# Mixture of softmaxes on one core: joint head weights, own buffers for the exponentials, and part loads of two heads

## Chip, core, metric

The kernel runs on one core of one Trainium2 chip. The metric is device time in microseconds (us) of one execution; each figure is the median of a kernel's runs. Each kernel ran in turns with the kernel before, on one chip. Three chips were used, with medians of the kernel before of 782.82, 782.70 and 782.74 us, and the control of the experiments (the changed kernel) ran on the first only; so where a run from another chip is set against the control, about 0.1 us of the difference may be the chip's. Two runs of one kernel mostly differ by 0.1 to 0.5 us.

## The reference

```python
def reference(logits, prior):            # logits (32, 128, 4, 4096), prior (32, 128, 4), float32
    prior_probs = softmax(prior, axis=-1)
    softmax = softmax(logits, axis=-1)   # over the vocabulary of 4096
    return np.sum(prior_probs[..., None] * softmax, axis=2)     # sum over the 4 heads
```

(The two softmaxes are written out in the original, with the maximum subtracted.) 268.5 MB come in and 67.1 MB go out.

## The kernel before

The 4096 rows are worked in 32 units of 128 rows. A unit loads 4 heads x 4096 values for each row (8.39 MB), takes exponentials on ScalarE, weights and adds them on VectorE, and stores 2.10 MB. There are two load buffers. Units 0 and 29 to 31 are loaded head by head, the others in one transfer.

```python
def pieces(b):
    return 1 if b == 0 or b >= B - 3 else H      # heads in one transfer
...
for b in range(B):
    ...
    if 0 < b < B - 3:
        store(b - 1, eng=nc.scalar)               # ahead of this unit's exponentials
    for h in range(H):
        et = lt[:, h] if inplace else ebuf[:, h % 2]          # two exponential buffers
        ex = nc.scalar.activation(et, lt[:, h], AF.Exp, accum_out=dsum[:, col])
        ...
        nc.vector.reciprocal(rden[:, col], dsum[:, col])      # one for each head
        if h == 0:
            nc.vector.tensor_scalar(out=acc, in0=et, scalar1=rden[:, col], scalar2=pp[...], ...)
            continue
        nc.gpsimd.tensor_mul(coeff[:, col], rden[:, col], pp[...])   # one for each head
        ...                                                   # last head of all: two halves
            nc.vector.scalar_tensor_tensor(out=acc[:, cs], in0=et[:, cs], scalar=coeff[:, col],
                                           in1=acc[:, cs], op0=ALU.mult, op1=ALU.add)
            if split:
                store(b, c * w, (c + 1) * w)
    if b + 2 < B:
        load(b + 2)                               # free once the four exponentials are done
```

The softmax here doesn't subtract the row's maximum and nothing guards it: scores larger than these inputs give would overflow.

Of the kernel before, what the change touches and what calls it, by code (L numbers as in the profile page):

```python
# [38 lines left out]
def kernel(  # L39
# [6 lines left out]
    nc = tc.nc  # L46
    B, S, H, V = logits.shape
    assert prior.shape == (B, S, H)
    assert out.shape == (B, S, V)
    P = 128  # L50
# [3 lines left out]
    B = G * J  # L54
    assert G * R == B * S and G <= 32

# [4 lines left out]
    lpool = ctx.enter_context(tc.tile_pool(name="lpool", bufs=2))  # L61
    apool = ctx.enter_context(tc.tile_pool(name="apool", bufs=2))
    cpool = ctx.enter_context(tc.tile_pool(name="cpool", bufs=1))


    def pieces(b):
        return 1 if b == 0 or b >= B - 3 else H

    ltiles = {}

    def load(b, eng=nc.sync):
        lt = lpool.tile([P, H, V], FP32, name="ltile")
        n = pieces(b)
        for h in range(0, H, n):
            eng.dma_start(out=lt[:, h : h + n], in_=lg[b // J, b % J, :, h : h + n, :])  # L75
        ltiles[b] = lt

    accs = {}

    def store(b, lo=0, hi=V, eng=nc.sync):  # L80
        eng.dma_start(out=ov[b // J, b % J, :, lo:hi], in_=accs[b][:, lo:hi])

    load(0, eng=nc.sync)
    nc.at_finalize(early_first_load)


    pr = cpool.tile([G, R, H], FP32, name="pr")
    nc.scalar.dma_start(out=pr, in_=pv)
    load(1, eng=nc.sync)
    pn = cpool.tile([32, H, R], FP32, name="pn")  # L90
    nc.gpsimd.memset(pn, 0.0)  # L91
    pmax = cpool.tile([G, R], FP32, name="pmax")
    nc.vector.reduce_max(pmax, pr, axis=AX.X)  # L93
    nc.vector.tensor_sub(pr, pr, pmax.unsqueeze(2).to_broadcast([G, R, H]))  # L94
    nc.scalar.activation(pr, pr, AF.Exp)  # L95
    nc.vector.reduce_sum(pmax, pr, axis=AX.X)  # L96
    nc.vector.reciprocal(pmax, pmax)  # L97
    nc.vector.tensor_mul(  # L98
        pn[0:G].rearrange("g h r -> g r h"), pr, pmax.unsqueeze(2).to_broadcast([G, R, H])
    )  # L100
    pq = pn.rearrange("g h (p j) -> g j h p", j=J)

    pp = cpool.tile([P, J, H, 32], FP32, name="pp")
    for t in range(P // 32):
        nc.vector.transpose(pp[32 * t : 32 * (t + 1)], pq[:, :, :, 32 * t : 32 * (t + 1)])  # L105

    NCHUNK = 2


    dsum = cpool.tile([P, B * H], FP32, name="dsum")  # L110
    rden = cpool.tile([P, B * H], FP32, name="rden")
    coeff = cpool.tile([P, B * H], FP32, name="coeff")


    ebuf = cpool.tile([P, 2, V], FP32, name="ebuf")

    exps = []

    for b in range(B):
        last = b == B - 1  # L120
        inplace = b >= B - 2
        lt = ltiles.pop(b)
        if not inplace:
            accs[b] = apool.tile([P, V], FP32, name="acc")
        else:
            accs[b] = lt[:, 0]
        acc = accs[b]
        if 0 < b < B - 3:
            store(b - 1, eng=nc.scalar)
        for h in range(H):  # L130
            split = last and h == H - 1
            i = b * H + h
            col = slice(i, i + 1)
            et = lt[:, h] if inplace else ebuf[:, h % 2]
            ex = nc.scalar.activation(et, lt[:, h], AF.Exp, accum_out=dsum[:, col])  # L135
            if h == 0:
                tc.keep_in_program_order(ex)


            if not inplace:  # L140
                if len(exps) >= 2:
                    tc.declare_no_dep(ex.ins, exps[-2], reason="covered by the sum")
                exps.append(ex.ins)
            nc.vector.reciprocal(rden[:, col], dsum[:, col])  # L144
            if h == 0:
                nc.vector.tensor_scalar(  # L146
                    out=acc, in0=et, scalar1=rden[:, col], scalar2=pp[:, b % J, h, b // J : b // J + 1],
# [51 lines left out]
```

## Time and profile before

| | |
|---|---|
| time, at first | 782.52 us (782.52 to 782.69, 3 runs) |
| span of the profiled run | 780.6 us |
| VectorE / ScalarE / POOL busy | 68% / 60% / 2% |
| transfers | nine tenths or more of every slice but the last |

The prediction below shows the lines and how to read them. The page's queue list: its columns are the queue and its kind, the packets, their MB, and their share of the 16 transfer engines' time.

```profile
q14 instruction: 7, 0.06, 0.0%
```

Seven packets of 8 KB each, in the whole run: instructions being fetched. 0.0% of the transfer time looks like nothing.

### The profile page before, as it was taken

The page shows a single profiled execution, that of the slowest core. Times are in us where ns is not written, and L with a number is a line of the kernel's source. Part 1 is how long each engine was busy: PE and PEld are TensorE (multiplying, and loading weights), DVE is VectorE, ACT ScalarE, POOL GpSimd, SP SyncE. Part 2 cuts the span into 40 slices and gives each one's busy share as a digit, 9 for nine tenths or more (in the row PEclk, how much of TensorE's full clock was granted, in tenths as well). Part 3 has the DMA queues.
Part 4 walks back from the last instruction along what each step waited for, and adds up shares of the span by engine and source line. Part 5 has one row for each costly group of instructions (what it writes and reads, how often), then busy time and mean ns, then how long its engine had stood idle before and what let it go on. Part 6 is the DMA issues. An engine that isn't in the chain of part 4 may idle for free.

```text
span 780.6 us, 853 instructions
## 1 busy us (share of the span) xinstructions
DVE 531.4 (68%) x266; ACT 470.2 (60%) x258; POOL 19.3 (2%) x101
## 2 busy tenths in 40 slices
DVE  5756668656686666866667765677666776668994
ACT  4376555755557655576555775457655567558971
POOL 0000000000000000000000000000000000000000
DMA  9999999999999999999999999999999999999998
GB/s 388 434 454 433 403 470 403 467 407 442 431 415 458 413 460 403 453 421 460 413 442 444 400 459 413 453 424 449 411 456 417 453 416 424 449 413 430 429 429 359
DMA packets 11127, 335.67 MB, mean 430 GB/s; under 512 B 1248, under 2 KB 1248, under 8 KB 1264
## 3 DMA queue, kind: packets, MB, share of 16 engines
q1 hardware_dynamic: 7056, 276.83, 82.2%
q10 hardware_dynamic: 4064, 58.79, 17.6%
q14 instruction: 7, 0.06, 0.0%
HBM read 268.50 MB, written 67.11 MB: 430 GB/s over the span
## 4 chain that ended last, share of the span: by engine, by line
DMA 66%; ACT 14%; DVE 10%; issue 7%; POOL 0%; SPq 0%; DVEq 0%; POOLq 0%; ACTq 0%
DMA ltile<-in_logits_dram 66%; ACT ebuf L135 14%; DVE acc L156 9%; DVE ltile L156 1%; POOL coeff L151 0%; SPq L75 0%; DVE rden L144 0%; DVEq L194 0%; DVE ltile L146 0%; POOLq L194 0%; ACTq L135 0%
## 5 line engine op out<-in xcount | busy, mean ns | idle before, releaser
L135 ACT ACTIVATE ebuf<-ltile 128x4096 f32<-128x4096 f32 x120 | 433.0, 3609 | 281.3 <-DMA ltile<-in_logits_dram 234.5
L156 DVE SCALAR_TENSOR_TENSOR acc<-ebuf,coeff,acc 128x4096 f32<-128x4096 f32 x90 | 403.6, 4484 | 27.3 <-POOL coeff L151 27.3
L144 DVE RECIPROCAL rden<-dsum 128x1 f32<-128x1 f32 x128 | 20.4, 160 | 200.7 <-ACT ebuf L135 200.7
L146 DVE TENSOR_SCALAR acc<-ebuf,rden,pp 128x4096 f32<-128x4096 f32 x30 | 72.4, 2412 | 1.1
L151 POOL TENSOR_TENSOR coeff<-rden,pp 128x1 f32<-128x1 f32 x96 | 18.2, 189 | 746.2 <-DVE rden L144 746.2
L135 ACT ACTIVATE ltile<-ltile 128x4096 f32<-128x4096 f32 x8 | 28.9, 3609 | 4.2 <-DMA ltile<-in_logits_dram 4.2
L156 DVE SCALAR_TENSOR_TENSOR ltile<-ltile,coeff 128x4096 f32<-128x4096 f32 (+1 forms) x7 | 27.0, 3874 | 1.8 <-POOL coeff L151 1.8
L135 ACT ACTIVATION_READ_ACCUMULATOR ebuf<-ltile 128x1 f32 x120 | 22.4, 186 | 0.0
L93 DVE TENSOR_REDUCE pmax<-pr 16x256 f32<-16x1024 f32 x1 | 1.2, 1207 | 7.0 <-DMA pr<-in_prior_dram 7.0
L95 ACT ACTIVATE pr<-pr 16x1024 f32<-16x1024 f32 x1 | 1.1, 1056 | 7.0 <-DVE pr L94 7.0
L146 DVE TENSOR_SCALAR ltile<-ltile,rden,pp 128x4096 f32<-128x4096 f32 x2 | 4.8, 2414 | 0.1
L98 DVE TENSOR_TENSOR pn<-pr,pmax 16x1024 f32<-16x1024 f32 x1 | 1.9, 1945 | 0.1
L95 ACT ACT_TABLE_LOAD x1 | 1.3, 1283 | 1.2 <-PEq L183 1.2
L96 DVE TENSOR_REDUCE pmax<-pr 16x256 f32<-16x1024 f32 x1 | 1.2, 1207 | 1.1 <-ACT pr L95 1.1
L105 DVE STREAM_TRANSPOSE pp<-pn 32x256 f32<-32x256 f32 x4 | 1.7, 435 | 0.1
L97 DVE RECIPROCAL pmax<-pmax 16x256 f32<-16x256 f32 x1 | 1.7, 1741 | 0.0
L135 ACT ACTIVATION_READ_ACCUMULATOR ltile<-ltile 128x1 f32 x8 | 1.5, 186 | 0.0
L94 DVE TENSOR_TENSOR pr<-pr,pmax 16x1024 f32<-16x1024 f32 x1 | 1.2, 1214 | 0.0
L91 POOL MEMSET pn<- 32x1024 f32 x1 | 0.9, 941 | 0.3 <-POOLq L183 0.3
L183 POOL MEMSET const-float32-0.0<- 128x1 f32 x1 | 0.1, 103 | 0.2 <-issue 0.2
L183 POOL MEMSET const-bfloat16-1.0<- 128x1 bf16 x1 | 0.1, 106 | 0.0
L183 POOL MEMSET const-uint8-127<- 128x1 uint8 x1 | 0.1, 106 | 0.0
(1 smaller groups left out, 0.1 us busy)
## 6 DMA issues: line engine op xcount, KB each, us to landing
out_dram<-acc ACTq DMA_DIRECT2D x28, 2048.0 KB, 29.3
ltile<-in_logits_dram SPq DMA_DIRECT2D x16, 2048.0 KB, 20.3
out_dram<-acc SPq DMA_DIRECT2D x2, 2048.0 KB, 32.9
out_dram<-ltile SPq DMA_DIRECT2D x1, 2048.0 KB, 21.2
out_dram<-ltile SPq DMA_DIRECT2D x2, 1024.0 KB, 8.7
ltile<-in_logits_dram SPq DMA_DIRECT2D x28, 32.3
pr<-in_prior_dram ACTq DMA_DIRECT2D x1, 64.0 KB, 6.2
```

The source lines that it names most:

```text
L93: nc.vector.reduce_max(pmax, pr, axis=AX.X)
L94: nc.vector.tensor_sub(pr, pr, pmax.unsqueeze(2).to_broadcast([G, R, H]))
L95: nc.scalar.activation(pr, pr, AF.Exp)
L96: nc.vector.reduce_sum(pmax, pr, axis=AX.X)
L97: nc.vector.reciprocal(pmax, pmax)
L98: nc.vector.tensor_mul(pn[0:G].rearrange("g h r -> g r h"), pr, pmax.unsqueeze(2).to_broadcast([G, R, H]))
L105: nc.vector.transpose(pp[32 * t : 32 * (t + 1)], pq[:, :, :, 32 * t : 32 * (t + 1)])
L135: ex = nc.scalar.activation(et, lt[:, h], AF.Exp, accum_out=dsum[:, col])
L144: nc.vector.reciprocal(rden[:, col], dsum[:, col])
L146: nc.vector.tensor_scalar(out=acc, in0=et, scalar1=rden[:, col], scalar2=pp[:, b % J, h, b // J : b // J + 1], op0=ALU.mult, op1=ALU.mult,)
L151: nc.gpsimd.tensor_mul(coeff[:, col], rden[:, col], pp[:, b % J, h, b // J : b // J + 1])
L156: nc.vector.scalar_tensor_tensor(out=acc[:, cs], in0=et[:, cs], scalar=coeff[:, col], in1=acc[:, cs], op0=ALU.mult, op1=ALU.add,)
```

## The change

Intent: fewer instructions and fewer waits. One reciprocal and one POOL product serve all four heads of a unit (two heads in the last four units). The first exponential is written in place, the other three have a buffer each (one in PSUM), so ScalarE does not wait for VectorE within a unit. A list of needed waits replaces those that the framework would insert. Loads in parts come as two heads, the last unit as two, one and one. The store of a unit now stands before the fourth exponential of the next one.

```diff
-        n = pieces(b)
-        for h in range(0, H, n):
-            eng.dma_start(out=lt[:, h : h + n], in_=lg[b // J, b % J, :, h : h + n, :])
+        if u == 0 or u >= U - 3:
+            cuts = (0, 2, 3, 4) if u == U - 1 else (0, 2, 4)
+        else:
+            cuts = (0, H)
+        for h, to in zip(cuts, cuts[1:]):
+            ld = nc.sync.dma_start(out=ltile[:, u % 2, h:to], in_=lg[u // J, u % J, :, h:to, :])
+            if u >= 2:
+                only(ld, adds[u - 2, 0] if h == 0 else exps[u - 2, to - 1])
 ... (cut: only() keeps just the named waits of an instruction)
-    ebuf = cpool.tile([P, 2, V], FP32, name="ebuf")
+    ebuf1 = cpool.tile([P, V], FP32, name="ebuf1")
+    ebuf2 = psum.tile([P, V], FP32, name="ebuf2")
+    ebuf3 = cpool.tile([P, V], FP32, name="ebuf3")
+            es = (lt[:, 0], ebuf1, ebuf2, ebuf3) if bufd else [lt[:, h] for h in range(H)]
 ...
-            nc.vector.reciprocal(rden[:, col], dsum[:, col])
-            nc.gpsimd.tensor_mul(coeff[:, col], rden[:, col], pp[:, b % J, h, b // J : b // J + 1])
+                rc = nc.vector.reciprocal(rden[:, u, h : h + n], dsum[:, u, h : h + n])
+                only(rc, exps[u, h + n - 1])
+                mul = nc.gpsimd.tensor_mul(
+                    coeff[:, u, h : h + n], rden[:, u, h : h + n], ppu[:, h : h + n]
+                )
 ...
+            m = H if u < U - 4 else 2                      # heads weighted together
+            for h in range(H):
+                if h == H - 1 and 0 < u < U - 3:
+                    store(u - 1, obuf[:, (u - 1) % 2], nc.scalar)
+                exp(h, ...)
+                if (h + 1) % m:
+                    continue
 ... (cut: weigh the m heads, add them one by one, last head of all in two halves)
```

More of the change, by code (lines that the diff above doesn't have):

```diff
@@ L46 @@
     nc = tc.nc
+    nc.at_finalize(early_first_load)
     B, S, H, V = logits.shape
@@ L53 @@
     G = B * S // R
-    B = G * J
-    assert G * R == B * S and G <= 32
+    U = G * J
+    assert G * R == B * S and G <= 32 and H == 4
     lg = logits.rearrange("b s h v -> (b s) h v").rearrange("(g p j) h v -> g j p h v", p=P, j=J)
@@ L59 @@
     pv = prior.rearrange("b s h -> (b s) h").rearrange("(g r) h -> g r h", r=R)
-    lpool = ctx.enter_context(tc.tile_pool(name="lpool", bufs=2))
-    apool = ctx.enter_context(tc.tile_pool(name="apool", bufs=2))
     cpool = ctx.enter_context(tc.tile_pool(name="cpool", bufs=1))
-    def pieces(b):
-        return 1 if b == 0 or b >= B - 3 else H
-    ltiles = {}
-    def load(b, eng=nc.sync):
-        lt = lpool.tile([P, H, V], FP32, name="ltile")
-        n = pieces(b)
-        for h in range(0, H, n):
-            eng.dma_start(out=lt[:, h : h + n], in_=lg[b // J, b % J, :, h : h + n, :])
-        ltiles[b] = lt
@@ L78, with only @@
-    accs = {}
-    def store(b, lo=0, hi=V, eng=nc.sync):
-        eng.dma_start(out=ov[b // J, b % J, :, lo:hi], in_=accs[b][:, lo:hi])
-    load(0, eng=nc.sync)
-    nc.at_finalize(early_first_load)
+    psum = ctx.enter_context(tc.tile_pool(name="psum", bufs=1, space=bass.MemoryType.PSUM))
+    before = {}
+    def only(ins, *keep):
+        for k in keep:
+            tc.add_manual_dep(
+                ins.ins,
+                k.ins.name,
+                mybir.DependencyInfo(mybir.DependencyClass.Sync, mybir.DependencyReason.DATA),
+                reason="all that this instruction waits for",
+            )
+        tc.declare_no_dep(
+            ins.ins,
+            group="loop",
+            keep=[k.ins for k in keep] + before.get(ins.ins.engine, []),
+            reason="covered by the waits that are kept",
+        )
+        tc.add_to_no_dep_group("loop", ins.ins)
+        before[ins.ins.engine] = [ins.ins]
+        return ins
@@ new lines, with load @@
+    ltile = cpool.tile([P, 2, H, V], FP32, name="ltile")
+    loads = {}
+    exps = {}
+    adds = {}
+    stores = {}
+    def load(u):
+        if u == 0 or u >= U - 3:
[3 more added lines that the diff above has]
+        for h, to in zip(cuts, cuts[1:]):
+            ld = nc.sync.dma_start(
+                out=ltile[:, u % 2, h:to], in_=lg[u // J, u % J, :, h:to, :]
+            )
+            if u >= 2:
+                only(ld, adds[u - 2, 0] if h == 0 else exps[u - 2, to - 1])
+            else:
+                only(ld)
+            for k in range(h, to):
+                loads[u, k] = ld
@@ L87, with store @@
+    def store(u, acc, eng, lo=0, hi=V):
+        st = eng.dma_start(out=ov[u // J, u % J, :, lo:hi], in_=acc[:, lo:hi])
+        stores[u] = only(st, adds[u, H - 1])
     pr = cpool.tile([G, R, H], FP32, name="pr")
-    nc.scalar.dma_start(out=pr, in_=pv)
-    load(1, eng=nc.sync)
     pn = cpool.tile([32, H, R], FP32, name="pn")
-    nc.gpsimd.memset(pn, 0.0)
     pmax = cpool.tile([G, R], FP32, name="pmax")
-    nc.vector.reduce_max(pmax, pr, axis=AX.X)
-    nc.vector.tensor_sub(pr, pr, pmax.unsqueeze(2).to_broadcast([G, R, H]))
@@ L95 @@
-    nc.scalar.activation(pr, pr, AF.Exp)
-    nc.vector.reduce_sum(pmax, pr, axis=AX.X)
-    nc.vector.reciprocal(pmax, pmax)
-    nc.vector.tensor_mul(
-        pn[0:G].rearrange("g h r -> g r h"), pr, pmax.unsqueeze(2).to_broadcast([G, R, H])
-    )
-    pq = pn.rearrange("g h (p j) -> g j h p", j=J)
-    pp = cpool.tile([P, J, H, 32], FP32, name="pp")
-    for t in range(P // 32):
-        nc.vector.transpose(pp[32 * t : 32 * (t + 1)], pq[:, :, :, 32 * t : 32 * (t + 1)])
-    NCHUNK = 2
-    dsum = cpool.tile([P, B * H], FP32, name="dsum")
@@ L111 @@
-    rden = cpool.tile([P, B * H], FP32, name="rden")
-    coeff = cpool.tile([P, B * H], FP32, name="coeff")
-    ebuf = cpool.tile([P, 2, V], FP32, name="ebuf")
-    exps = []
-    for b in range(B):
-        last = b == B - 1
-        inplace = b >= B - 2
-        lt = ltiles.pop(b)
-        if not inplace:
-            accs[b] = apool.tile([P, V], FP32, name="acc")
-        else:
-            accs[b] = lt[:, 0]
-        acc = accs[b]
-        if 0 < b < B - 3:
-            store(b - 1, eng=nc.scalar)
-        for h in range(H):
-            split = last and h == H - 1
-            i = b * H + h
-            col = slice(i, i + 1)
-            et = lt[:, h] if inplace else ebuf[:, h % 2]
-            ex = nc.scalar.activation(et, lt[:, h], AF.Exp, accum_out=dsum[:, col])
-            if h == 0:
-                tc.keep_in_program_order(ex)
-            if not inplace:
-                if len(exps) >= 2:
-                    tc.declare_no_dep(ex.ins, exps[-2], reason="covered by the sum")
-                exps.append(ex.ins)
-            nc.vector.reciprocal(rden[:, col], dsum[:, col])
-            if h == 0:
-                nc.vector.tensor_scalar(
-                    out=acc, in0=et, scalar1=rden[:, col], scalar2=pp[:, b % J, h, b // J : b // J + 1],
-                    op0=ALU.mult, op1=ALU.mult,
-                )
-                continue
-            nc.gpsimd.tensor_mul(coeff[:, col], rden[:, col], pp[:, b % J, h, b // J : b // J + 1])
-            n = NCHUNK if split else 1
-            w = V // n
-            for c in range(n):
-                cs = slice(c * w, (c + 1) * w)
-                nc.vector.scalar_tensor_tensor(
-                    out=acc[:, cs], in0=et[:, cs], scalar=coeff[:, col], in1=acc[:, cs],
-                    op0=ALU.mult, op1=ALU.add,
-                )
-                if split:
-                    store(b, c * w, (c + 1) * w)
-        if b + 2 < B:
-            load(b + 2)
-        if b == B - 3:
-            store(b - 1)
-            store(b)
-        elif b == B - 2:
-            store(b)
@@ new lines, with exp, weigh, add @@
+    pp = cpool.tile([P, J, H, 32], FP32, name="pp")
+    dsum = cpool.tile([P, U, H], FP32, name="dsum")
+    rden = cpool.tile([P, U, H], FP32, name="rden")
+    coeff = cpool.tile([P, U, H], FP32, name="coeff")
+    ebuf1 = cpool.tile([P, V], FP32, name="ebuf1")
+    ebuf2 = psum.tile([P, V], FP32, name="ebuf2")
+    ebuf3 = cpool.tile([P, V], FP32, name="ebuf3")
+    obuf = cpool.tile([P, 2, V], FP32, name="obuf")
+    with tc.manual_schedule():
+        load(0)
+        nc.scalar.dma_start(out=pr, in_=pv)
+        load(1)
+        nc.gpsimd.memset(pn, 0.0)
+        nc.vector.reduce_max(pmax, pr, axis=AX.X)
+        nc.vector.tensor_sub(pr, pr, pmax.unsqueeze(2).to_broadcast([G, R, H]))
+        nc.scalar.activation(pr, pr, AF.Exp)
+        nc.vector.reduce_sum(pmax, pr, axis=AX.X)
+        nc.vector.reciprocal(pmax, pmax)
+        nc.vector.tensor_mul(
+            pn[0:G].rearrange("g h r -> g r h"), pr, pmax.unsqueeze(2).to_broadcast([G, R, H])
+        )
+        pq = pn.rearrange("g h (p j) -> g j h p", j=J)
+        for t in range(P // 32):
+            nc.vector.transpose(pp[32 * t : 32 * (t + 1)], pq[:, :, :, 32 * t : 32 * (t + 1)])
+        for u in range(U):
+            bufd = u < U - 2
+            lt = ltile[:, u % 2]
+            acc = obuf[:, u % 2] if bufd else lt[:, 0]
+            es = (lt[:, 0], ebuf1, ebuf2, ebuf3) if bufd else [lt[:, h] for h in range(H)]
+            ppu = pp[:, u % J, :, u // J]
+            def exp(h, *keep):
+                ex = nc.scalar.activation(
+                    es[h], lt[:, h], AF.Exp, accum_out=dsum[:, u, h : h + 1]
+                )
+                keep = (loads[u, h],) + keep
+                if bufd and h and u:
+                    keep += (adds[u - 1, h],)
+                exps[u, h] = only(ex, *keep)
+            def weigh(h, n, *keep):
+                rc = nc.vector.reciprocal(rden[:, u, h : h + n], dsum[:, u, h : h + n])
+                only(rc, exps[u, h + n - 1])
+                mul = nc.gpsimd.tensor_mul(
+                    coeff[:, u, h : h + n], rden[:, u, h : h + n], ppu[:, h : h + n]
+                )
+                return only(mul, rc, *keep)
+            def add(h, mul, lo=0, hi=V):
+                if h == 0:
+                    st = nc.vector.tensor_scalar(
+                        out=acc[:, lo:hi], in0=es[h][:, lo:hi], scalar1=coeff[:, u, h : h + 1],
+                        scalar2=None, op0=ALU.mult,
+                    )
+                    adds[u, h] = only(st, mul)
+                else:
+                    st = nc.vector.scalar_tensor_tensor(
+                        out=acc[:, lo:hi], in0=es[h][:, lo:hi], scalar=coeff[:, u, h : h + 1],
+                        in1=acc[:, lo:hi], op0=ALU.mult, op1=ALU.add,
+                    )
+                    adds[u, h] = only(st, mul, adds[u, h - 1])
+            free = (stores[u - 2],) if bufd and u >= 2 else ()
+            m = H if u < U - 4 else 2
+            for h in range(H):
+                late = h == H - 1 and 4 <= u < U - 3
+                if h == H - 1 and 0 < u < U - 3:
+                    store(u - 1, obuf[:, (u - 1) % 2], nc.scalar)
+                exp(h, *((stores[u - 4],) if late else ()))
+                if (h + 1) % m:
+                    continue
+                g = h + 1 - m
+                mul = weigh(g, m, *(free if g == 0 else ()))
+                for k in range(g, h + 1):
+                    n = 2 if u == U - 1 and k == H - 1 else 1
+                    w = V // n
+                    for c in range(n):
+                        add(k, mul, c * w, (c + 1) * w)
+                        if n > 1:
+                            store(u, acc, nc.sync, c * w, (c + 1) * w)
+            if u + 2 < U:
+                load(u + 2)
+            if u == U - 3:
+                store(u - 1, obuf[:, (u - 1) % 2], nc.sync)
+                store(u, acc, nc.sync)
+            elif u == U - 2:
+                store(u, acc, nc.sync)
```

## The prediction

> **What bounds the kernel now.** I read the page first: busy shares, then the transfer lines, then the chain of work that ended last.
>
> ```profile
> span 780.6 us, 853 instructions
> DVE 531.4 (68%) x266; ACT 470.2 (60%) x258; POOL 19.3 (2%) x101
> DMA  9999999999999999999999999999999999999998
> DMA packets 11127, 335.67 MB, mean 430 GB/s; under 512 B 1248, under 2 KB 1248, under 8 KB 1264
> DMA 66%; ACT 14%; DVE 10%; issue 7%; POOL 0%; SPq 0%; DVEq 0%; POOLq 0%; ACTq 0%
> ```
>
> No compute engine is above 68%, while the transfer row is at nine tenths from the first slice to the last but one. 268.5 MB of logits must come in and 67.1 MB of result go out, whatever the order of the arithmetic; the change moves the same bytes. Next I asked for the transfers of two whole units in the middle (a unit is 128 rows: an 8.39 MB load and a 2.10 MB store), from one unit's first exponential to that of the second after it.
>
> ```profile
> DMA packets 577, 20.98 MB, mean 433 GB/s; under 512 B 64, under 2 KB 64, under 8 KB 64
> q1 hardware_dynamic: 288, 16.78, 80.0%
> q10 hardware_dynamic: 288, 4.19, 20.2%
> out_dram<-acc ACTq DMA_DIRECT2D x2, 2048.0 KB, 29.3
> ltile<-in_logits_dram SPq DMA_DIRECT2D x2, 32.3
> ```
>
> Two units take 48.35 us, 24.17 each, and the shares add to 100%: the engines never rest. A load lands 32.3 us after its issue though a unit lasts 24.17, so each load is queued some 8.1 us before the one ahead has landed. That 8.1 us is the slack of the chain "landed, exponentials, issue into the freed buffer". The timeline of that unit shows it:
>
> ```profile
> 332.32 3.62 ACT L135 ACTIVATE ebuf<-ltile 128x4096 f32<-128x4096 f32 x1 [8.14 <-DMA ltile<-in_logits_dram]
> 344.64 3.62 ACT L135 ACTIVATE ebuf<-ltile 128x4096 f32<-128x4096 f32 x1 [1.42 <-DVE acc L156]
> 348.38 24.50 SPq L75 DMA_DIRECT2D ltile<-in_logits_dram  x2
> 354.37 0.34 ACTq L81 DMA_DIRECT2D out_dram<-acc  x1
> 356.49 3.62 ACT L135 ACTIVATE ebuf<-ltile 128x4096 f32<-128x4096 f32 x1 [8.14 <-DMA ltile<-in_logits_dram]
> ```
>
> Call 332.32 T, the landing. The next load goes out at T+16.06; ScalarE then idles 8.14 us for data. The 1.42 us wait for VectorE within the unit only eats slack. So the middle is transfer-bound, and what may change the time is the two ends. The tail:
>
> ```profile
> 760.19 3.62 ACT L135 ACTIVATE ltile<-ltile 128x4096 f32<-128x4096 f32 x1 [1.17 <-DMA ltile<-in_logits_dram]
> 761.28 4.48 DVE L156 SCALAR_TENSOR_TENSOR ltile<-ltile,coeff 128x4096 f32<-128x4096 f32 x1 [0.30 <-POOL coeff L151]
> 766.15 4.61 DVE L156 SCALAR_TENSOR_TENSOR ltile<-ltile,coeff 128x2048 f32<-128x2048 f32 x2 [0.30 <-POOL coeff L151]
> 768.52 2.60 SPq L81 DMA_DIRECT2D out_dram<-ltile  x2
> DMA  8997998999799989974221321211100000000000
> ```
>
> The last head lands at 760.2, and the last two half-stores are issued at 768.5 and 770.8. The last row (40 slices of 774 to 781) stays full until about 777.2: even here the stores queued behind the loads keep the engines fed. That is why finer work at the end would have been worth nothing before, and why later work there could cost.
>
> **What the Trainium skill says.** "DMA: Bandwidth & Descriptors", Specifications, puts the fabric ceiling at 435 GB/s; the middle's 433 agrees, so no room is left. Its lower HBM limit of about 358 per core does not hold here, and the measurement decides. The same page, Queues, rings and completion order, says that each transfer engine alternates between the rows that have work, packet by packet. The trace agrees: 288 packets on each of the two queues in the two units, 80% to 20% of the time. Hence a 2 MB store takes as long as an 8 MB load beside it (29.3 us), and when one queue runs dry the other takes its place. "VectorE: DVE Perf Modes", Why PSUM operands drop a tier, says that a PSUM operand caps fp32 at the basic rate. The PSUM buffer of the third head is read only by the two-tensor add, which at 4484 ns for 4096 elements is 1.09 ns an element; I estimate that it is at that rate already, and expect no change.
>
> **The change part by part.**
> Fewer instructions. Reciprocals go from 128 to 28+8=36, the small products on POOL from 96 to 36. At 160 ns and 189 ns that is 92 x 0.16 = 14.7 us of VectorE and about 11 us of POOL. The 0.30 us gap ahead of each add (27.3 us in sum) mostly goes too. All of it lies beside transfers: worth 0.
>
> Waits. Each head has its own exponential buffer (the first in place), so ScalarE no longer waits 44.6 us in sum for VectorE. Four exponentials back to back take 4 x 3.61 + 0.19 = 14.6 us instead of 16.0. But the first weighted product now waits for all four, and the next load waits for that product, since the first head is read from the load buffer: T + 14.6 + 0.16 + 0.19 + 0.1 of hand-over + 2.41 = T+17.5, to 17.7 with hand-overs. The load goes out 1.6 us later; slack falls from 8.1 to about 6.5. No cost.
>
> Stores. One unit's adds end 0.45 + 2.41 + 3 x 4.48 = 16.3 us after its exponentials, at T+31, which is 6.8 us into the next unit. The store of it stands before the fourth exponential of that unit, so it is issued between 7.3 and 10.9 us after that landing instead of 2.1 us before it (354.37 against 356.49). With the 29.3 us from above it lands 12.4 to 16.0 us into the second unit on. The POOL product there waits for it, at T+14.8: a wait of 0 to 1.2 us. The load then goes out by T+18.9, with 5.3 us of slack. A late store does not build up: adds 16.3 + store 29.3 = 45.6 us, less than two units' 48.35.
>
> Start. Unit 0 in two parts: its first exponential starts when 4.2 MB have landed, about 12 us instead of 10.4. The third load goes out near 32 instead of 28.5, and unit 1 is not in before 43.4. Nothing lost.
>
> Tail. Two-head parts and two-head weights delay the end. If the loads land as before (750.5, 755.3, 760.2 for the three parts of the last unit), exponentials of unit 31 end at 754.1, 757.7, 761.3 and 764.9. The adds of its heads 0 and 1 start at 758.3 and end at 765.2; the joint weights of heads 2 and 3 come at 765.7. Then 4.48 for head 2 (770.2), 2.35 for each half of head 3: stores at 772.6 and 774.9, 4.1 us later than before. Did the engines have other work? In the row above the data ends near 777.2. The last unit's 2.1 MB take 4.85 us at 432 GB/s, so the store of unit 30 ends near 772.3. In the kernel before, the first load's packets begin 1.0 us after its issue, so the first half-store moves from about 773.6: the engines rest 1.3 us. Its 1 MB lasts to 776.0; the second half (774.9 + 1.0) just fits. So the data ends near 778.5 instead of 777.2.
>
> Sum: 0 + 0 + 0 + 1.3 us. 782.5 + 1.3 = 783.8; I take 783.6, for the seven transfers saved (16 part loads become 9) and their 16 completion packets each.
>
> **The rivals.**
> A: gain in the middle. The removed waits (44.6 us, 27.3 us) and 26 us of small instructions look like several per cent. For it speak only the engines' idle times; against it the full transfer row. At the middle's 433 GB/s 335.67 MB take 775.2 us, so the span cannot fall by more than 5.4 us: 777 at best, 0.7% off.
> B: the new wait of the product for the store two units back, with the load behind it, starves the load queue. For it: only 2.3 us to -1.2 us of margin at the product, and the largest store latency in the trace is 33.5 us. Then the load goes out at T+23, about 1 us before the landing. Against it: a dry load queue hands the engines to the store, which then lands sooner. If each of 28 units still lost 0.3 us: 8 us, 791.
> C: the delayed tail is hidden after all, if more store data is left at the end than before. Then 782.5, or a little less for fewer transfers: 782.
> D: the tail is worse than worked out, if ScalarE or VectorE drift behind in the last four units: each us of delay beyond 772.6 costs a full us. 2 us more: 785.5.
>
> **Range and chances.** C gives the lower side, D the upper, B a thin tail beyond. 80% range: 781.5 to 787. Over 2% faster is below 767, under the transfer floor: 0.01. Over 2% slower is above 798.5, and needs 0.5 us lost in each unit: 0.03. Within 2%: 0.96.
>
> **What would show it.** Right: a transfer row full at 433 GB/s in the middle with units 24.17 us apart; ScalarE's waits for VectorE gone and its waits for loads longer by as much; loads issued 17.5 to 19 us after a landing; the store's issue 7 to 11 us after it; the last half-stores near 772.6 and 774.9 with a dip in the transfer row just before. Wrong: gaps in the transfer row in the middle with waits of the POOL product for a store (B), a rate above 435 GB/s (A), or no dip at the end (C).

## The result, and the profile after

| | before | after |
|---|---|---|
| median | 782.68 us (782.52 to 782.79, 6 runs) | 781.02 us (780.92 to 781.08, 6 runs) |
| span of the profiled run | 780.55 us | 779.28 us |

Ratio 0.9979, 95% interval 0.9966 to 0.9992. (A ratio is the mean of one kernel's fast runs over the mean of the other's of the same rounds, so not quite the ratio of the medians.) By the 2% rule it is the same; but it is a gain of 1.66 us, where I had said a loss of 1.1 and a range from 781.5 up. The result lies 0.5 us below that range.

The page of the kernel after, the same lines as before with the instruction queue:

```profile
span 779.3 us, 654 instructions
DVE 521.0 (67%) x174; ACT 466.7 (60%) x258; POOL 8.3 (1%) x41
DMA packets 10117, 335.66 MB, mean 431 GB/s; under 512 B 1136, under 2 KB 1136, under 8 KB 1152
q14 instruction: 5, 0.04, 0.0%
```

199 instructions fewer, the same bytes, and two instruction fetches fewer. Counted by engine with its waits and transfer issues, the trace has 311 instructions before and 181 after for VectorE, 324 and 294 for ScalarE, 115 and 83 for POOL, 97 and 90 for SyncE. Of the 199, 92 are reciprocals, 60 are POOL products, 7 are load issues, and 40 are waits (net).

The transfers of the kernel after in the same window in the middle, 48.4 us long:

```profile
DMA packets 577, 20.99 MB, mean 434 GB/s; under 512 B 64, under 2 KB 64, under 8 KB 64
q1 hardware_dynamic: 288, 16.78, 80.0%
q10 hardware_dynamic: 289, 4.21, 20.3%
out_dram<-obuf ACTq DMA_DIRECT2D x2, 2048.0 KB, 29.4
ltile<-in_logits_dram SPq DMA_DIRECT2D x2, 30.9
```

The same packets and pace; stores land after 29.4 us as before, loads after 30.9 instead of 32.3, for they are issued later. And the timeline of a unit in the kernel after (start, duration, engine, line, operation; in brackets the idle time ahead of it and what ended it):

```profile
330.69 3.62 ACT L159 ACTIVATE ltile<-ltile 128x4096 f32<-128x4096 f32 x1 [9.67 <-DMA ltile<-in_logits_dram]
337.49 0.34 ACTq L113 DMA_DIRECT2D out_dram<-obuf  x1
348.10 24.50 SPq L100 DMA_DIRECT2D ltile<-in_logits_dram  x2
354.86 3.62 ACT L159 ACTIVATE ltile<-ltile 128x4096 f32<-128x4096 f32 x1 [9.67 <-DMA ltile<-in_logits_dram]
```

Units are 24.17 us apart, as before. The load goes out 17.41 us after the landing (predicted 17.5 to 17.7), the store 6.80 after it (predicted 7.3 to 10.9: ScalarE's queue reaches it while the second exponential runs). ScalarE idles 9.67 us for data instead of 8.14: what the removed waits gave back went there. That the landing comes 1.6 us earlier than before (330.69 for 332.32) is no gain yet: stores go out later in a unit, so at any time more load data and less store data has been moved. The packet records of both traces, added up at ten times between 90 and 690 us, show the same sum to within 0.13 MB (0.3 us).

So the difference must be at the end. The transfer row of 774 to 781 us, 40 slices of 0.175 us in tenths of the 16 engines, of the kernel after; that of the kernel before is in the prediction:

```profile
DMA  8959799996959899832211000000000000000000
```

Both rows fall from full near 777, and then there is a foot. It is two to four engines that finish alone: until 779.2 before, until 778.0 after. The timeline of the kernel after at its end:

```profile
749.22 3.62 ACT L159 ACTIVATE ltile<-ltile 128x4096 f32<-128x4096 f32 x1 [2.41 <-DMA ltile<-in_logits_dram]
764.29 9.13 DVE L183 SCALAR_TENSOR_TENSOR ltile<-ltile,coeff 128x4096 f32<-128x4096 f32 x3 [0.31 <-POOL coeff L170]
771.19 2.60 SPq L113 DMA_DIRECT2D out_dram<-ltile  x2
```

The last half-stores go out at 771.2 and 773.5. I had said 772.6 and 774.9, because the last unit's first part landed at 749.2 and not at 750.5.

A transfer of 128 rows is spread over 16 engines, each with its own packets and one small completion packet at the end. I took the times of these completion packets from the trace, 16 for each transfer, and sorted them. All of this comes from one profiled run of each kernel. This is the table that the rest rests on (us from the start of the span; "typical" is the median of the 16 engines). Unit 30's store is the last one but for the two halves:

```
                            fetches  store of unit 30 done on     last packet   span    time
                            (q14)    typical     last engine      of all                (median)
before                       7       772.45      774.27           779.17        780.55  782.68
after                        5       772.07      773.06           777.96        779.28  781.02
```

Two things moved. The typical engine is 0.38 us earlier, and the last engine, which ends the kernel, is no longer 1.82 us but 0.99 us behind it: 0.83 us. Together 1.21 of the 1.27 us of the span. From the store of unit 30 to the end the last engine takes 4.90 us in both kernels: on it there was no rest in the tail.

**Why are some engines late?** Followed through the run, the lag of the engine that ends last does not creep up: it jumps, at the times of the q14 packets, and stays. Here are two engines of the kernel before, in us behind the first, at the ends of successive loads:

```
load ends at            137.5   161.7   185.8  ...  451.8   476.0   500.2   524.4
engine A (last of all)  0.15    0.99    0.99        0.99    0.99    1.83    1.83
engine B                0.04    0.04    0.59        0.59    1.15    1.15    1.15
fetches between         146.7   164.7               470.6   486.1
```

(Which row is which engine is inferred: the records name no engine. Of the other 14 lags twelve hardly move here. One jumps by 0.5 us at the fetch of 349.2. One creeps without a fetch, from 0.1 at 114 us to 0.9 at 735; why is not known.) A fetch is a packet of 8 KB that takes 0.309 us, and the data packet behind it on the same engine is longer than its usual 2.42 us: 2.66 us after the fetches at 164.7 and 470.6, 2.95 us after those at 146.7 and 486.1. So one fetch costs its engine 0.55 or 0.84 us, and since every engine has its full share of data queued until the end, it never catches up. The Trainium skill's page "DMA: Bandwidth & Descriptors", Queues, rings and completion order, lists row 14 as internal to the runtime, with refills among its uses; that fits the trace's name for it.

Read in the same way, the kernel after has two fetches on its last engine (147.9 and 511.1), of 0.55 us each: 0.11, 0.66, 1.22 us behind the first. The engine with the 0.84 us fetch that is left (194.0) ends 1.08 behind and is no longer last. One fetch fewer for VectorE is not enough by this reading: before, the next engine ended only 0.13 us ahead of the last (1.93 for 2.06 behind the first), after two fetches of 0.55 and a late one of 0.7 (749.7). I take that engine's fetches for ScalarE's; it lost the third one too, with 30 waits fewer in ScalarE's stream.

Theory L (lag): the end is set by the slowest transfer engine, whose lag is the sum of the instruction fetches that pass through it; fewer instructions are fewer fetches. Rivals: P, the parts make the gain; S, the later stores make it; W, the shorter weights and missing waits as such.

### The profile page after: what moved, and what is told of

Read it like the earlier page. It is cut to its first block, busy times and chain, and to the rows that moved or that the text cites. A ratio compares the mean times of both kernels' runs of the same rounds, so it can differ in the third digit from the quotient of the medians.

```text
span 779.3 us, 654 instructions
## 1 busy us (share of the span) xinstructions
DVE 521.0 (67%) x174; ACT 466.7 (60%) x258; POOL 8.3 (1%) x41
## 4 chain that ended last, share of the span: by engine, by line
DMA 64%; ACT 27%; DVE 6%; issue 2%; POOL 0%; DVEq 0%; POOLq 0%
DMA ltile<-in_logits_dram 62%; ACT ebuf L159 19%; ACT ltile L159 8%; DVE obuf L177 5%; DMA out_dram<-obuf 2%; DVE ltile L183 1%; POOL coeff L170 0%; DVE rden L168 0%; DVEq L240 0%; POOLq L240 0%; POOLq L170 0%
## 5 line engine op out<-in xcount | busy, mean ns | idle before, releaser
L183 DVE SCALAR_TENSOR_TENSOR obuf<-ebuf,coeff,obuf 128x4096 f32<-128x4096 f32 x90 | 403.6, 4484 | 3.8 <-POOL coeff L170 0.6
L159 ACT ACTIVATE ebuf<-ltile 128x4096 f32<-128x4096 f32 x90 | 322.9, 3589 | 7.4 <-DMA ltile<-in_logits_dram 7.4
L159 ACT ACTIVATE ltile<-ltile 128x4096 f32<-128x4096 f32 x38 | 137.3, 3614 | 280.6 <-DMA ltile<-in_logits_dram 280.6
L168 DVE RECIPROCAL rden<-dsum 128x4 f32<-128x4 f32 (+1 forms) x36 | 6.3, 175 | 227.9 <-ACT ebuf L159 225.1
L177 DVE TENSOR_SCALAR obuf<-ltile,coeff 128x4096 f32<-128x4096 f32 x30 | 70.6, 2353 | 10.2 <-POOL coeff L170 10.2
L159 ACT ACTIVATION_READ_ACCUMULATOR ebuf<-ltile 128x1 f32 x90 | 16.8, 186 | 0.0
L170 POOL TENSOR_TENSOR coeff<-rden,pp 128x4 f32<-128x4 f32 (+1 forms) x36 | 7.2, 200 | 755.3 <-DVE rden L168 745.4
L159 ACT ACTIVATION_READ_ACCUMULATOR ltile<-ltile 128x1 f32 x38 | 7.1, 186 | 0.0
L177 DVE TENSOR_SCALAR ltile<-ltile,coeff 128x4096 f32<-128x4096 f32 x2 | 4.7, 2354 | 0.6 <-POOL coeff L170 0.6
## 6 DMA issues: line engine op xcount, KB each, us to landing
out_dram<-obuf ACTq DMA_DIRECT2D x28, 2048.0 KB, 29.4
ltile<-in_logits_dram SPq DMA_DIRECT2D x2, 2048.0 KB, 30.9
ltile<-in_logits_dram SPq DMA_DIRECT2D x28, 30.9
```

Of the source, the lines that this page charges most:

```text
L159: ex = nc.scalar.activation(es[h], lt[:, h], AF.Exp, accum_out=dsum[:, u, h : h + 1])
L168: rc = nc.vector.reciprocal(rden[:, u, h : h + n], dsum[:, u, h : h + n])
L170: mul = nc.gpsimd.tensor_mul(coeff[:, u, h : h + n], rden[:, u, h : h + n], ppu[:, h : h + n])
L177: st = nc.vector.tensor_scalar(out=acc[:, lo:hi], in0=es[h][:, lo:hi], scalar1=coeff[:, u, h : h + 1], scalar2=None, op0=ALU.mult,)
L183: st = nc.vector.scalar_tensor_tensor(out=acc[:, lo:hi], in0=es[h][:, lo:hi], scalar=coeff[:, u, h : h + 1], in1=acc[:, lo:hi], op0=ALU.mu ...
```

## Experiments

Eleven kernels ran, in rounds of 5. All gave correct results but one. The common table is at the end of this section.

**Control.** The changed kernel again, no edit.

> The changed kernel once more, as the control of this chip. Every theory: 781.0 us (780.8 to 781.2) beside 782.7 of the kernel before. Theory L (lag): the end is set by the slowest of the 16 transfer engines; each 8 KB fetch of instructions that passes through one of them (queue 14) puts that engine 0.35 to 0.85 us behind for good, and the change drops one VectorE fetch from the engine that was last. L expects 5 fetches again and the last engine 0.9 to 1.3 us behind the first at the end. Theory P (parts): the gain comes from 9 part loads in place of 16. Theory S (stores): the gain comes from stores that go out later in a unit, behind more load data.

781.06 us (780.91 to 781.1), 5 fetches, last engine 0.92 us behind the typical one (0.97 behind the first at the end). As expected.

**504 fills on POOL.** Does a fetch alone cost time? POOL is idle 99% of the time and its fills are on nobody's path.

```diff
+    pad = cpool.tile([P, 512], FP32, name="pad")
+            for k in range(18 if u < 28 else 0):
+                only(nc.gpsimd.memset(pad[:, 18 * u + k : 18 * u + k + 1], 0.0))
```

> The changed kernel with 504 one-element fills on POOL, which is idle 99% of the time. L: four more fetches (9), all for POOL and so through one transfer engine, about 0.55 us each; that engine ends 2.4 to 3 us behind the first, time 782.4 us (781.8 to 783.5). P and S: 781.0 (780.8 to 781.2).

782.73 us (782.7 to 782.81): 1.67 us more than the control. Fills of one element that nobody waits for took back the whole gain. The page of this kernel:

```profile
span 780.9 us, 1158 instructions
DVE 530.8 (68%) x174; ACT 466.7 (60%) x258; POOL 24.9 (3%) x545
q14 instruction: 9, 0.07, 0.0%
```

POOL is still 97% idle. The typical engine finishes unit 30's store at 772.09, as in the control (772.16); the last one at 774.70, where it was 773.08. The records show one engine fall back by 0.53 to 0.61 us at each of four fetches. The end of the kernel moved by the same 1.6 us. P and S are not needed for this loss, and it shows that lag of one engine is enough.

**1008 fills on POOL.** The same edit with 36 for each unit.

> The changed kernel with 1008 one-element POOL fills, double those of the earlier run, which cost 1.67 us. L: eight more fetches than the changed kernel (13), all on one transfer engine at about 0.6 us each: 4.8 to 5.4 us behind, time 784.5 to 785.5 us: each further four fetches cost 2.4 us. If the earlier loss was a one-off of POOL being busy, less than 783.5.

785.68 us (785.04 to 786.01), 4.62 us over the control, a little above the expected range. (4.3 us of it lie in the span; the rest is outside, see the end of the next section.) 12 fetches in the span, not 13, seven more than in the control. Eight of them are POOL's; the packets behind them take 2.63 to 2.75 us, so 0.52 to 0.64 us each, and the last engine is 5.0 us behind the typical one. The transfer row of this kernel, 770 to 780 us:

```profile
DMA  1949949366130300101001010076999879977999
```

From 772.7 to 776.5 only one engine, or a few, work and the others have nothing: a load counts as landed only when its last engine is done, so the last unit's arithmetic, and with it the last stores, start late for all. That makes the last engine's lag the delay of the whole tail.

**92 fills on VectorE.** As many as the change took reciprocals away.

```diff
+            for k in range(3 if u < 28 else 2):
+                only(nc.vector.memset(pad[:, i : i + 1], 0.0))
```

> The changed kernel with 92 one-element VectorE fills in it, as many as it has fewer reciprocals, at places where VectorE idles. L: VectorE's second fetch is back (6 fetches), the slowest engine ends 1.7 to 2.1 us behind the first, time 781.9 us (781.6 to 782.3). P and S: nothing on the path changes, 781.0 (780.8 to 781.2).

781.15 us (781.13 to 781.24). L missed: 6 fetches came as expected, but the cost was 0.1 us and not 0.9. The trace tells why. The two VectorE fetches, at 135.6 and 523.2, this time had a short store packet (16 KB) behind them, not a 64 KB load packet; it was stretched by 0.34 us instead of 0.53, so each fetch cost 0.65 us and not 0.84. The last engine was 1.31 us behind the typical one, which itself was 0.33 us ahead of that of the control (771.83 to 772.16). The number of fetches alone does not fix the lag; what stands behind each in the queue does too.

**348 fills on VectorE.** After that miss, a larger dose: 12 for each of 29 units.

> The changed kernel with 348 one-element VectorE fills of 0.06 us at places where VectorE idles: 21 us of idle time used, nothing on the path. Theory L (each instruction fetch puts one transfer engine behind for good): four VectorE fetches in place of one, 0.55 to 0.85 us each on one engine, which is 2.4 to 3.6 us behind the first at the last store but one instead of 1.2; time 782.2 to 783.4 us. A theory in which fills cost nothing expects 781.05. The run with 92 fills showed only 0.1 us; if the number of fetches doesn't matter, it is 0.4 here by its instructions.

783.49 us (783.36 to 783.6), at the upper end and just above it. 8 fetches, four of them VectorE's, each with a load packet behind it that took 2.95 to 3.03 us: 0.84 or 0.92 us each, 3.5 in sum. The last engine is 3.54 us behind the typical one, whose own time (772.08) is that of the control.

**Single weights in the changed kernel.** One reciprocal and one product for each head again.

```diff
-            m = H if u < U - 4 else 2
+            m = 1
-                only(ld, adds[u - 2, 0] if h == 0 else exps[u - 2, to - 1])
+                only(ld, exps[u - 2, to - 1], *((adds[u - 2, 0],) if h == 0 else ()))
```

> The changed kernel with one reciprocal and one POOL product for each head, as before the change: 92 more of each; parts, buffers and the places of the stores stay as in the changed kernel. L: VectorE has two fetches again and POOL one more, slowest engine 1.7 to 2.1 us behind, time 781.9 us (781.6 to 782.3), as in the run with 92 fills. P and S: 781.0. A theory that joint weights gain by their shorter chain would also expect a loss here, but none in the run with the fills.

781.64 us (781.43 to 781.78), 0.58 us slower than the control. The direction and roughly the size are L's (6 fetches, though L expected 7); the last engine is 1.68 us behind the typical one. P and S expected 781.0. Taken by the times alone, a loss here and hardly any with 92 fills is what rival W, the shorter weights as such, foretells. The records speak for L: VectorE's stream has 273 instructions in both runs and two fetches in both, but here both have a load packet behind them (2.95 us each), so they cost 0.84 us and not 0.65. That accounts for the 0.37 us by which the last engine lags more (1.68 for 1.31); the typical engine is no later than in the control (771.85 for 772.16). Joint weights are thus worth some 0.6 us here, by way of the lag.

**All reciprocals out of the kernel before** (wrong result).

```diff
-            nc.vector.reciprocal(rden[:, col], dsum[:, col])
-  scalar1=rden[:, col]     nc.gpsimd.tensor_mul(coeff[:, col], rden[:, col], pp[...])
+  scalar1=dsum[:, col]     nc.gpsimd.tensor_mul(coeff[:, col], dsum[:, col], pp[...])
```

> The kernel before without any of its 128 reciprocals; the sums stand in their place, so the result is wrong on purpose. If fewer instructions gain in proportion, 128 gain at least 1.3 us of the 1.66 that the change gained with 184 fewer: 781.4 or less. L: VectorE's second fetch goes, but ScalarE's three fetches stay and their engine was only 0.1 us ahead of the last one, so the next-to-last engine sets the end: 782.5 us (782.3 to 782.7) beside 782.7.

782.23 us (782.12 to 782.43) beside 782.74. The proportional theory fails. L's range (782.3 to 782.7) was missed by 0.1 us, and its reason was wrong. The page of this kernel:

```profile
span 780.6 us, 816 instructions
q14 instruction: 7, 0.06, 0.0%
```

128 reciprocals are gone, but only 37 instructions: others took their place. The trace shows which: VectorE's semaphore waits rose from 42 to 133, so its stream still has 274 instructions (311 before). Both VectorE fetches are still there (174.8 and 562.5), and the span of this profiled run is that of the kernel before. Over all runs the spans have a median of 780.4 us beside 780.6: 0.2 us of the gain of 0.5 are in the span, and 0.3 outside of it (see the end of the next section).

**Two-head parts in the kernel before.**

```diff
-        for h in range(0, H, n):
-            eng.dma_start(out=lt[:, h : h + n], in_=lg[b // J, b % J, :, h : h + n, :])
+        cuts = (0, H) if pieces(b) == H else (0, 2, 3, 4) if b == B - 1 else (0, 2, 4)
+        for h, to in zip(cuts, cuts[1:]):
+            eng.dma_start(out=lt[:, h:to], in_=lg[b // J, b % J, :, h:to, :])
```

> The kernel before with nothing changed but the parts: units loaded in parts come in two-head parts, the last unit as two, one and one. Theory P (the parts make the gain): 781.1 us. Theory L (the slowest transfer engine, late by its instruction fetches): the count of instructions stays, so does the last engine's lag of about 2.0 us; only the pace of the part loads gains, 0.2 to 0.5 us: 782.4 us (782.2 to 782.6) beside 782.8.

781.99 us (781.71 to 781.99) beside 782.7: ratio 0.999, interval 0.9976 to 1.0004. More than L's 782.2, less than P's 781.1. In the trace the typical engine is 0.34 us earlier and the span 0.53 us shorter. Over all runs the spans differ by 0.4 us (medians 780.2 and 780.6), and 0.3 us of the gain lie outside the span. Nor did the instructions stay as they were: 838 for 853, with 6 fetches in the span for 7, and the last engine 0.13 us less behind.

**Single-head parts in the kernel after.**

```diff
-            cuts = (0, 2, 3, 4) if u == U - 1 else (0, 2, 4)
+            cuts = (0, 1, 2, 3, 4)
```

> The changed kernel with single-head parts again (16 part loads instead of 9), all else kept. P: 782.7 us. L: 781.4 us (781.2 to 781.6), the last engine still 1.0 to 1.3 us behind.

781.55 us median (781.37 to 782.9), 0.5 us over the control; the typical engine 0.17 us later than in the control, the span 0.49 us longer. P expected 1.7. From both sides the parts are worth about 0.5 us in the span. The single runs do not overlap with those that they are compared with (781.99 at most to 782.55 at least; 781.37 at least to 781.10 at most), but the 95% interval of the first ratio includes 1, and these runs spread widely. P, that the parts are the whole gain, fails.

**A late tail.** One fill of a whole row on VectorE just ahead of the two last half adds.

```diff
+                    if n > 1:
+                        only(nc.vector.memset(ebuf1, 0.0))
```

> The changed kernel with one VectorE fill of 4096 elements (1.1 or 2.2 us, D below) just ahead of the two last half adds, so that the two last half-stores go out D later. If all 16 engines are alike, as the prediction had it, they already idle before these stores and each us of D costs a full us: 781.05 + D. L: the engine that ends last is still busy with the store before for about 0.85 us after the first half-store could begin on the early engines, so the time is 781.05 + D - 0.85.

785.09 us (784.94 to 785.19). The fill was longer than I had thought: 3.47 us. The timeline of this kernel, and its transfer row of 770 to 780 us:

```profile
769.58 3.47 DVE L205 MEMSET ebuf<- 128x4096 f32 x1 [0.80 <-issue]
772.97 4.48 DVE L183 SCALAR_TENSOR_TENSOR ltile<-ltile,coeff 128x2048 f32<-128x2048 f32 x2
```

```profile
DMA  9499696603000000000000009988899789998799
```

The store issues at 775.22 came 4.03 us later than in the changed kernel (771.19), so D is 4.0. "All engines alike" gives 785.1, which is what was measured; L gave 784.2. Taken at the time, the experiment speaks for the view that L denies. The records say why. The last engine's first half-store was done 3.36 us later than in the changed kernel (778.87 for 775.51), the typical one's 4.03 us later: the last engine had indeed 0.67 us to spare. But the last instruction fetch, which in the changed kernel came at 774.8, came at 778.9, behind the rest, and put the last engine from 0.31 to 0.74 us behind the first at the very end. And 0.2 us of the time are outside the span (2.0 us for 1.8 in the changed kernel). So 4.03 - 0.67 + 0.43 + 0.23 = 4.02 us: by this account the agreement with "all engines alike" is accidental. The account is made after the fact, from the packet times; no run left out that fetch.

**A finer tail.** Heads 2 and 3 of the last unit weighted apart, the last head in four quarters.

```diff
+                fine = u == U - 1 and h >= 2
-                g = h + 1 - m
-                mul = weigh(g, m, *(free if g == 0 else ()))
+                g = h if fine else h + 1 - m
+                mul = weigh(g, 1 if fine else m, *(free if g == 0 else ()))
-                    n = 2 if u == U - 1 and k == H - 1 else 1
+                    n = 4 if u == U - 1 and k == H - 1 else 1
```

> The changed kernel with a finer end: heads 2 and 3 of the last unit weighted apart and the last head added and stored in four quarters, so that the first store data of it is ready about 1.5 us earlier. If all 16 engines are alike, the rest of 0.3 to 0.4 us before the last store vanishes: 780.7 us. L: the engine that ends last never rested there, so no gain: 781.05 (780.9 to 781.2).

781.43 us (781.27 to 781.79), no gain; 0.37 us over the control and above L's range too (781.2). The 0.37 us are outside the span (2.16 us for 1.79): the spans of the five runs have the control's median, 779.3 us. The transfer row, 770 to 780 us:

```profile
DMA  9799697687999989999899998996411000000000
```

The row is full from 772 to the fall, so the early engines no longer rest there, and the end is not earlier: the last engine takes 5.09 us from unit 30's store to the end instead of 4.90. "All engines alike" (780.7, so 0.35 us less) fails. This was also the try for a version better than both; it is none, and the experiments point to no other with more than a few tenths to gain.

All kernels in one table, with the columns of the small one above:

```
                            fetches  store of unit 30 done on     last packet   span    time
                            (q14)    typical     last engine      of all                (median)
before                       7       772.45      774.27           779.17        780.55  782.68
before, two-head parts       6       772.11      773.80           778.71        780.02  781.99
before, no reciprocals       7       772.67      774.38           779.29        780.64  782.23
after                        5       772.07      773.06           777.96        779.28  781.02
after again                  5       772.16      773.08           777.99        779.27  781.06
after, 92 VectorE fills      6       771.83      773.14           778.05        779.37  781.15
after, 348 VectorE fills     8       772.08      775.62           780.52        781.81  783.49
after, 504 POOL fills        9       772.09      774.70           779.60        780.95  782.73
after, 1008 POOL fills      12       772.74      777.72           782.63        783.92  785.68
after, single weights        6       771.85      773.53           778.44        779.82  781.64
after, single-head parts     5       772.33      773.38           778.29        779.76  781.55
after, late tail             5       772.09      773.09           781.78        783.17  785.09
after, finer tail            5       772.02      773.03           778.12        779.42  781.43
```

In all but the two last rows the end of all packets is 4.90 to 4.91 us after the last engine's end of unit 30's store. The last engine's column alone gives the end of the kernel; the typical engine's does not.

## Why the prediction was wrong, point by point

- *What bounds the kernel; rival A.* Right. Units stayed 24.17 us apart at 434 GB/s, and 44.6 us of removed ScalarE waits turned into waits for loads.
- *Waits and stores in the middle; rival B.* Right: 17.41 us for the load's issue. POOL's product waited for a store just once, in unit 29, and was then late by 0.8 us.
- *Fewer instructions: "worth 0".* This step failed. It is true of the engines that execute the instructions. It missed that instructions are themselves fetched through the transfer engines, which are the bound. The page showed the line (seven packets on q14), and I passed over it because of its 0.0%. The last engine's lag on the typical one fell from 1.82 to 0.99 us: -0.83 us. The runs with POOL fills show that the mechanism is enough by itself: 4 more fetches, +1.67 us; 7 more, eight of them POOL's, +4.62 us.
- *Tail: "the engines rest 1.3 us".* This step failed too. It is the larger of the two, and it alone gave the forecast its sign. It took 16 engines for one: "the store of unit 30 ends near 772.3" is the typical engine's end (772.45), while the last engine was busy with that store until 774.27. A first half-store at 773.6 would have found it busy even if the loads had landed as before. In fact they landed 1.3 us earlier (a landing waits for the last engine, which was 0.83 us less behind, and the typical one was 0.38 us earlier). From unit 30's store to the end the first engine took 5.17 us instead of 4.91, the typical one 5.01 instead of 4.91, the last one 4.90 as before. So the rest was 0.26, 0.1 and 0 us, and only the last of these counts. Rival C (782, the tail hidden) came nearest, but for another reason than the one it gave: the store data left was the same. After the last load three whole stores and two halves remained in both kernels, and they took 19.5 us on the last engine in both.
- *Parts: 0.2 us for seven transfers saved.* Somewhat too small: about 0.5 us of the span by the two runs (0.34 us of it on the typical engine in one, 0.17 in the other).
- *Sum.* Said: +1.1 us. Measured in the span: -0.83 (lag) - 0.38 (typical engine) + 0 (tail) = -1.21, with -0.06 from the last packet to the end of the span, -1.27.

What stays open. The time fell by 1.66 us, the span by 1.27. In the profiled runs the time is longer than the span by 2.12 us before and 1.79 after; over all kernels this part is either 1.78 to 1.79 or 2.02 to 2.16, with no pattern I could tie to the change (the kernel before without reciprocals has 1.79, the finer tail 2.16). It is no noise: this part was 2.08 to 2.17 in every run of the kernel before beside the experiments and 1.73 to 1.84 in every run of the changed one. So some 0.3 us of the gain are outside all that the packets show, and the 0.2 and 0.3 us that some experiments have there say nothing for or against L.

The typical engine's 0.38 us are explained in part only: the parts account for 0.17 to 0.34, and this engine's end moves by 0.3 us between builds with the same parts (771.83 to 772.16). S was not tested by itself: no run put the stores back to their old place. Against it stand only the unchanged pace and the equal sums of data in the middle.

Nor did I find out why a fetch stretches the packet behind it, and why by 0.53 us or more for one engine's instructions and by 0.24 for another's. And the split of the 0.83 us is from reading the traces: three engines end late before (1.4 to 1.8 us behind the typical one), after the fetches that I take for VectorE's two, ScalarE's three and one of another (the last on the engine that had crept); no run took away just one of them.

## What to carry to other kernels

When the transfer engines are full from end to end, ask which of the 16 ends last, and not how full they are on average: the foot of the transfer row after its fall shows it. What passes through one engine, even 8 KB of instructions, is paid at the end if it falls on the engine that ends last, so a long unrolled program can have a price though its instructions are hidden. Waits are instructions too: count them with the arithmetic. An end game that is worked out with the mean engine can be wrong by more than it is worth.

## What the Trainium skill lacked or had wrong

- "Runtime: NRT & Kernel Launch", Instruction fetch mechanics, gives refills in 16 KiB blocks of 256 instructions, at a cost "mostly hidden". Here each fetch is one packet of 8,192 bytes. With 1008 POOL fills, 37 POOL instructions a unit, fetches came about every 3.4 units, so some 128 instructions each (an estimate from these two numbers). Hidden they were from the engine that executes, not from the transfers: 0.52 to 0.92 us for the transfer engine concerned with a load packet behind the fetch (0.309 us of fetch and 0.21 to 0.61 on the packet behind), and 1.67 us of kernel time for four.
- "DMA: Bandwidth & Descriptors", Queues, rings and completion order, lists row 14 but no cost of its packets to the other rows. The page's section Why a DMA increments its semaphore by 16 and not by 1 does say that a transfer's engines finish independently; the size of that was 0.9 to 5.0 us between the typical and the last engine here.
- The same page, Specifications, gives the HBM limit of about 358 GB/s for each core without a condition; its section Bandwidth says that this is each core's share when both cores of an HBM domain stream. So the 433 to 434 GB/s over two units in the middle, with one core running, don't contradict the page; the table, on which the prediction rested, lacks the condition.
- No page that I read tells that removing arithmetic may leave the instruction stream nearly as long: 128 reciprocals removed were 37 instructions fewer (853 to 816), with 91 more waits on VectorE (42 to 133), and no fetch fewer.
